# Two transformer blocks on one core: the second block's weight halves are made during the first block's feed-forward stage and kept in DRAM

## The chip, the cores and the metric

The kernel runs on one core of a Trainium2 chip. A core has five engines with an instruction queue each: TensorE (PE, matrix products; its weight loads are listed as PEld), VectorE (DVE), ScalarE (ACT), GpSimd (POOL) and SyncE (SP, which here only issues DMAs), and 16 DMA engines that all queues share. The metric is the device time of one execution in microseconds (us), the median of the runs.

## The reference

One sequence of 512 tokens of width 1024, all in float32, goes through two different transformer blocks:

```
def reference(x, ...):
    x = first_block(x, ...)       # window attention + sparse attention, merge, w_out;
                                  # then the feed-forward stage with w_ffn_in, conv, gate, w_ffn_out
    return second_block(x, ...)

# second_block
h = rms_norm(x, norm_g)
proj = h @ w_in                                        # [512, 2464]
cq, ckv, kr, dq, dk, dv, mq, z = split(proj, IN_OFFSETS_2)
y_mla  = mla_branch(cq, ckv, kr, ..., w_uq, w_ukv)     # 8 heads, latent attention (MLA)
y_diff = diff_branch(dq, dk, dv, ...)                  # 4 heads, two softmax maps each
y_mem  = mem_branch(mq, mem, ...)                      # 4 heads over 256 memory tokens
y = concat([y_mla, y_diff, y_mem]) * silu(z)
return x + y @ w_out                                   # w_out: [1024, 1024]
```

In the kernel the second block's weights are `w_in_2` (1024 x 2464), `w_uq_2` (256 x 768), `w_ukv_2` (128 x 1024) and `w_out_2` (1024 x 1024), 15.6 MB as float32.

## The kernel before, in words

TensorE multiplies in a 32-bit format that is narrower than float32 (float32r). So each float32 operand is split into two float32r halves, H (the rounded value) and L (the rest), and each product is three: H*H, H*L and L*H. `mm3` issues them (L193, L197, L198).

Weights take this way: `wload` has SP load a raw float32 tile into one of two `raw` buffers (L122); `wsplit` copies it to `wH` on ACT (L129) and subtracts to get `wL` on DVE or POOL, whichever `self.leng` names (L130). wH and wL have three buffers each of 128 x 1024. `dense_steps` computes transposed outputs, a tile of 128 features x 512 tokens at a time (24 products of 512 columns where the depth is 1024); `nat_steps` computes token-major outputs. Such tiles are collected in PSUM in two banks (tag `mm`, bufs=2), so a tile's result must be read out before the next but one begins.

The first block ends with its output product (`wo`) and the feed-forward stage `ffn`, in two halves: 11 pairs of u and g tiles of `w_ffn_in` each (22 tiles; DVE multiplies the PSUM bank by the token's factor at L959 (`cv`), a three-tap convolution follows on ACT and DVE (`cc`, L960 to L962), a gate and a split (`ct`, `aL`)), then eight tiles of `w_ffn_out` (`fo`).

The second block makes its latents (`lat`), stores the residual in token-major form, makes the queries and keys (`nat`, `uq`, `ukv`), norms and rotates them on DVE and POOL (`head_stat` L1060, `rsqrt` L267 to L274, `head_scale` L1069, `rope` L1090 on POOL, L1094 and L1096 on DVE), and runs three attentions, one behind the other in `pipeline`, with the gates `z` (eight tiles of 128 columns of `w_in_2`, L1464 to L1470) and the first half of the output product as fillers between their steps. The last half of the output product comes at the end. With `POOLL = 14`, `self.leng` is POOL from L1452 on and in the fillers of the attention, elsewhere DVE.

The program is written as generators that `weave` runs side by side; a scheduler then sets each engine's order from a list of priorities. On each engine, and on SP's queue, instructions run strictly in that order.

## Time and profile before

| | |
|---|---|
| runs | 1107.42, 1115.65, 1118.71 us; median 1115.65 |
| span of the profiled execution | 1107.7 us |
| mean clock granted to TensorE | 0.987 of full speed |
| busy in the span | PE 1049.2, DVE 759.3, ACT 579.9, POOL 267.8 us |
| HBM | 100.49 MB read, 10.77 MB written |

The median of the runs lies 8 us above the span of the profiled execution. By time, the first block's attention ends at about 396 us, its output product at 443, the feed-forward stage's first half at about 607, its second half at 803; the second block's latents and residual follow until 836, its queries and keys until 890, then the attentions until about 1071 and the end of the output product. Busy times are sums over an engine's instructions where they don't overlap; the share of busy time in the whole span hides that each stage has another limit, so the table by stretches is read stage by stage. "[5.34 <-POOL wL L130]" behind a row means that the engine was idle for 5.34 us before it, and what released it.

### The profile page before, as it was taken

Reading aid. Unit: us, or ns where it says so; the run is one execution under the profiler, and the core shown is the slowest. Engines: PE = TensorE matmul, PEld = TensorE weight load, DVE = VectorE, ACT = ScalarE, POOL = GpSimd, SP = SyncE. Lnnn points to the kernel's source line nnn. Section 1 sums busy time; section 2 is a strip of 40 time slices with the busy share of each in tenths; the row PEclk is TensorE's granted clock in tenths of the full one; section 3 lists DMA queues with packets and bytes.
Section 4 is the critical chain, followed back from the end, with each engine's and each line's share of the span. In section 5 each row is a group of like instructions: output and inputs, shape, how many; then the busy total and the mean of one; then the engine's idle time right before and its main releaser. Section 6 shows DMA issues by size and latency. Waiting matters only on the chain.

```text
span 1107.7 us, 15081 instructions
## 1 busy us (share of the span) xinstructions
PE 1049.2 (95%) x5425; PEld 872.8 (79%) x5425; DVE 759.3 (69%) x1553; ACT 579.9 (52%) x1098; POOL 267.8 (24%) x380
## 2 busy tenths in 40 slices
PE   5999989999999999999999999999999959999898
PEld 4797777877878878888888888888889947776688
DVE  6669884577872655777753477874454898988983
ACT  6557664577772444444432344445546527876640
POOL 4423134222220064000000200002410558331400
PEclk9999999999999999999999999999999979999999
DMA  7844345222114252232222423222333321264222
GB/s 184 273 115 156 100 102 136 43 48 43 49 44 113 77 181 88 76 114 84 83 81 78 151 90 101 76 81 79 110 97 109 96 57 39 89 179 143 68 66 77
DMA packets 105194, 110.14 MB, mean 99 GB/s; under 512 B 5508, under 2 KB 96106, under 8 KB 105120
## 3 DMA queue, kind: packets, MB, share of 16 engines
q1 hardware_dynamic: 101184, 98.81, 30.6%
q0 software_dynamic: 3936, 10.37, 3.1%
q8 instruction: 43, 0.70, 0.3%
q14 instruction: 31, 0.25, 0.1%
HBM read 100.49 MB, written 10.77 MB: 100 GB/s over the span
## 4 chain that ended last, share of the span: by engine, by line
PE 70%; DVE 15%; DMA 6%; ACT 4%; issue 3%; SPq 0%; POOL 0%; ACTq 0%; DVEq 0%; POOLq 0%
PE ps_mm L193 18%; PE ps_mm L197 18%; PE ps_mm L198 18%; DMA raw<-in_w_in 5%; PE ps_S L1241 3%; PE ps_T L383 3%; DVE wL L130 2%; PE ps_O L1272 1%; DMA xt<-in_x 1%; PE ps_O L1270 1%; DVE PTL L102 1%; ACT wH L129 1%; DVE e L372 1%; DVE rt L1094 1%; DVE e L1615 1%
## 5 line engine op out<-in xcount | busy, mean ns | idle before, releaser
L129 ACT ACTIVATE wH<-raw 128x1024 fp32r<-128x1024 f32 (+5 forms) x178 | 169.4, 953 | 260.9 <-PE ps_mm L197 207.8
L130 DVE TENSOR_TENSOR wL<-raw,wH 128x1024 fp32r<-128x1024 f32 (+5 forms) x150 | 166.6, 1112 | 116.5 <-ACT wH L129 116.1
L198 PE MATMUL ps_mm<-nH,wL 128*128 128x512 f32 x440 | 173.4, 394 | 5.3 <-POOL wL L130 5.3
L193 PE MATMUL ps_mm<-nH,wH 128*128 128x512 f32 x440 | 174.0, 395 | 0.0
L197 PE MATMUL ps_mm<-nL,wH 128*128 128x512 f32 x440 | 173.5, 394 | 0.0
L374 ACT ACTIVATE e<-e,mn 128x256 f32<-128x256 f32 (+5 forms) x160 | 86.4, 541 | 33.5 <-DVE mn L372 32.4
L198 PEld LDWEIGHTS ps_mm<-nH,wL 128*128 128x128 f32 x440 | 83.4, 189 | 22.6 <-POOL wL L130 5.8
L197 PEld LDWEIGHTS ps_mm<-nL,wH 128*128 128x128 f32 x440 | 83.5, 190 | 16.5
L193 PEld LDWEIGHTS ps_mm<-nH,wH 128*128 128x128 f32 x440 | 83.6, 190 | 16.2
L193 PE MATMUL ps_mm<-hH,wH 128*128 128x512 f32 x232 | 93.9, 405 | 0.0
L198 PE MATMUL ps_mm<-hH,wL 128*128 128x512 f32 x232 | 92.1, 397 | 0.0
L197 PE MATMUL ps_mm<-hL,wH 128*128 128x512 f32 x232 | 91.6, 395 | 0.0
L130 POOL TENSOR_TENSOR wL<-raw,wH 128x1024 fp32r<-128x1024 f32 (+1 forms) x28 | 60.8, 2170 | 76.5 <-ACT wH L129 63.3
L383 PE MATMUL ps_T<-ident,e 128*128 128x128 f32 x368 | 64.3, 282 | 11.4 <-DVE PTL L102 7.2
L101 ACT ACTIVATE PTH<-ps_T 128x512 fp32r<-128x512 f32 (+1 forms) x108 | 55.6, 528 | 32.6 <-PE ps_T L383 32.1
L102 DVE TENSOR_TENSOR PTL<-ps_T,PTH 128x512 fp32r<-128x512 f32 (+1 forms) x108 | 63.9, 606 | 12.3 <-ACT PTH L101 11.6
L193 PE MATMUL ps_mm<-aH,wH 128*128 128x512 f32 x176 | 69.5, 395 | 0.0
L198 PE MATMUL ps_mm<-aH,wL 128*128 128x512 f32 x176 | 69.5, 395 | 0.0
L197 PE MATMUL ps_mm<-aL,wH 128*128 128x512 f32 x176 | 69.5, 395 | 0.0
L383 PEld LDWEIGHTS ps_T<-ident,e 128*128 128x128 f32 x368 | 45.4, 143 | 28.7 <-DVE PTL L102 8.8
L958 POOL MEMSET cv<- 128x2 f32 x44 | 4.2, 99 | 237.1 <-DVE cc L962 230.5
L959 DVE TENSOR_TENSOR cv<-ps_mm,rB 128x512 f32<-128x512 f32 x44 | 30.3, 688 | 32.5 <-PE ps_mm L198 31.3
(550 smaller groups left out, 2544.0 us busy)
## 6 DMA issues: line engine op xcount, KB each, us to landing
raw<-in_w_ffn_in SPq DMA_DIRECT2D x20, 1024.0 KB, 5.2
raw<-in_w_in SPq DMA_DIRECT2D x16, 1024.0 KB, 6.9
raw<-in_w_in SPq DMA_DIRECT2D x16, 512.0 KB, 4.0
raw<-in_w_ffn_out SPq DMA_DIRECT2D x8, 768.0 KB, 4.7
raw<-in_w_ffn_out SPq DMA_DIRECT2D x8, 640.0 KB, 4.2
xt<-in_x SPq DMA_DIRECT2D x8, 512.0 KB, 4.9
raw<-in_w_out SPq DMA_DIRECT2D x4, 1024.0 KB, 5.2
raw<-in_w_out SPq DMA_DIRECT2D x8, 512.0 KB, 3.5
```

The lines of the kernel that those rows point to most:

```text
L101: nc.scalar.activation(H, src, AF.Copy)
L102: nc.vector.tensor_sub(L, src, f32(H))
L129: self.nc.scalar.activation(H, raw, AF.Copy)
L130: self.leng.tensor_sub(L, raw, f32(H))
L193: ins = mm(ps, wH, xH, start=first, stop=False)
L197: mm(ps, wH, xL, start=False, stop=False)
L198: mm(ps, wL, xH, start=False, stop=last)
L372: nc.vector.tensor_tensor_reduce(e, ps, bias, op0=ALU.add, op1=ALU.min, scale=1.0, scalar=3e38, accum_out=mn)
L374: nc.scalar.activation(e, e, AF.Exp, scale=-1.0, bias=mn, accum_out=sm)
L383: nc.tensor.transpose(ps[:, 128 * i:128 * i + 128], blk, self.ident)
L959: nc.vector.tensor_tensor(v[:, 2:], ps, rB, op=ALU.mult)
L1241: nc.tensor.matmul(ps[:, :n], q[:, 128 * b:128 * b + 128], k[:, :n], start=i == 0, stop=i == len(prods) - 1)
```

## The change

A list `later()` names 32 pieces of the second block's weights, mostly of 128 x 1024. A generator `presplit()` loads each into an SBUF tile `pre` (tag "e", two buffers, shared with the attention's strips), splits it in chunks of 512 columns into `preH` (ACT) and `preL` (DVE) with four buffers each, and stores both to DRAM, a piece later, 256 KB a store. `ffn` steps it behind gate and output tiles and drains it at the end. The second block then has no `wload` and `wsplit`: `fetch()` loads the ready halves from DRAM, for three of five pieces into wH and wL with a DMA each, for two of five into the two `raw` buffers with one DMA. `stream()` asks for a piece one ahead of its use (two ahead for the gates and the last half of the output product). The lines that set `self.leng` to POOL ahead of the attention are gone.

```
+    def presplit(self):
+        ...
+        def load(i):
+            key, n, w, pieces = specs[i]
+            t = self.work.tile([128, 1280], F32, tag="e", name="pre", bufs=2)[:, :n * w]
+            tv = t.rearrange("p (k c) -> p k c", k=n)
+            for o, pw, src in pieces:
+                nc.sync.dma_start(tv[:, :, o:o + pw], src)
+            return t
+        nxt = load(0)
+        yield
+        for i, (key, n, w, _) in enumerate(specs):
+            t = nxt
+            nxt = load(i + 1) if i + 1 < len(specs) else None
+            for d, st in ready:
+                nc.sync.dma_start(f32(d), f32(st))
+            ready = []
+            dst = self.dram.tile([128, 2, n * w], F32R, name="pre_" + "_".join(map(str, key)))
+            for o in range(0, n * w, 512):
+                m = min(512, n * w - o)
+                H = self.work.tile([128, 512], F32R, tag="PTH", name="preH", bufs=4)
+                L = self.work.tile([128, 512], F32R, tag="PTL", name="preL", bufs=4)
+                self.split(t[:, o:o + m], H[:, :m], L[:, :m])
+                ready += [(dst[:, 0, o:o + m], H[:, :m]), (dst[:, 1, o:o + m], L[:, :m])]
+            self.held[key] = (dst, n, w)
+            yield
+    def fetch(self, key):
+        dst, n, w = self.held.pop(key)
+        self.turn = getattr(self, "turn", -1) + 1
+        if self.turn % 5 < 3:
+            T = [self.wp.tile([128, n * w], F32R, tag=t, name=t, bufs=3) for t in ("wH", "wL")]
+            for i in range(2):
+                self.nc.sync.dma_start(f32(T[i]), f32(dst[:, i]))
+        else:
+            t = self.wp.tile([128, 2, n * w], F32R, tag="raw", name="wHL", bufs=2)
+            self.nc.sync.dma_start(f32(t), f32(dst))
+            T = [t[:, i] for i in range(2)]
+        return [t.rearrange("p (k c) -> p k c", k=n) for t in T]
...
     def ffn(self, last):
+            pre = self.presplit()
...
                     self.dense(Wi, [(0, 8)], 128 * (FT + i0 + i), 128 * n, self.nH, self.nL, gate)
+                    if hf or i > 2:
+                        next(pre)
+                        if i % 4:
+                            next(pre)
...
                     if hf:
                         last(m, x1)
+                    next(pre, None)
+                    if not hf:
+                        next(pre, None)
...
+            self.drain(pre)
...
-        if POOLL & 8:
-            self.leng = nc.gpsimd
...
-            yield from self.dense_steps(lambda k0, k1, c, w: W(k0, k1, 1440 + 128 * ZO[c // 128], w), [(0, 8)], 0, D,
-                                        self.nH, self.nL, ev, chunk=128)
+            yield from self.dense_steps(None, [(0, 8)], 0, D, self.nH, self.nL, ev, chunk=128,
+                                        pre=self.stream((("z", i) for i in range(8)), 2))
```

What this does to the order of instructions is seen at three places. On DVE in the feed-forward stage's first half, two u tiles stand like this before (`cv` reads the product out of PSUM, `cc` is the convolution, `wL` a half of the weights of the tile after):

```order
L959 TENSOR_TENSOR cv<-ps_mm,rB 128x512
L130 TENSOR_TENSOR wL<-raw,wH 128x1024
L961 SCALAR_TENSOR_TENSOR cc<-cv,vec_norm_ffn,cc 128x512
L962 SCALAR_TENSOR_TENSOR cc<-cv,vec_norm_ffn,cc 128x512
L959 TENSOR_TENSOR cv<-ps_mm,rB 128x512
```

and of the change, at the same place:

```order
L1057 TENSOR_TENSOR cv<-ps_mm,rB 128x512
L137 TENSOR_TENSOR wL<-raw,wH 128x1024
L1059 SCALAR_TENSOR_TENSOR cc<-cv,vec_norm_ffn,cc 128x512
L109 TENSOR_TENSOR preL<-pre,preH 128x512
L1060 SCALAR_TENSOR_TENSOR cc<-cv,vec_norm_ffn,cc 128x512
L109 TENSOR_TENSOR preL<-pre,preH 128x512
L1057 TENSOR_TENSOR cv<-ps_mm,rB 128x512
```

Two subtractions of a piece stand between a tile's `cv` and the next one's; in the 22 tiles there are 41.

On SP's queue in the same stage the loads of `w_ffn_in` follow each other in the kernel before, nine of 1 MB in a row:

```order
L122 DMA raw<-in_w_ffn_in 128x8x256
L908 DMA xt_3963<-in_x 128x4x256
L122 DMA raw<-in_w_ffn_in 128x8x256 x9
L122 DMA raw<-in_w_ffn_in 128x8x128 x2
L122 DMA raw<-in_w_ffn_out 128x6x256
```

and of the change, from one of these loads to behind the next:

```order
L129 DMA raw<-in_w_ffn_in 128x8x256
L191 DMA pre_nat_0_5587<-preL 128x512
L191 DMA pre_nat_0_5587<-preH 128x512
L191 DMA pre_nat_0_5587<-preL 128x512
L183 DMA pre<-in_w_in 128x4x256
L191 DMA pre_nat_4_5645<-preH 128x512
L191 DMA pre_nat_4_5645<-preL 128x512
L191 DMA pre_nat_4_5645<-preH 128x512
L191 DMA pre_nat_4_5645<-preL 128x512
L129 DMA raw<-in_w_ffn_in 128x8x256
L183 DMA pre<-in_w_in 128x4x256
```

A load and seven stores of pieces stand between two loads of the stage's own weights. The 124 stores in all are issued ahead of the first load of the feed-forward stage's second half.

On POOL where the queries `qn` and keys `kn` of the second block are rotated, the kernel before has weight halves between the rotation products:

```order
L130 TENSOR_TENSOR wL<-raw,wH 128x1024
L1090 TENSOR_TENSOR rt_7727<-qn,cc_mla_qn_g_5669 128x256
L1090 TENSOR_TENSOR rt_7746<-qn,cc_mla_qn_g_5669 128x256
L130 TENSOR_TENSOR wL<-raw,wH 128x1024
L1090 TENSOR_TENSOR rt_7769<-qn,cc_mla_qn_g_5669 128x256
L130 TENSOR_TENSOR wL<-raw,wH 128x1024 x2
L1090 TENSOR_TENSOR rt_7880<-kn,cc_mla_kn_g_5678 128x256
```

and of the change:

```order
L1197 TENSOR_TENSOR rt_8170<-qn,cc_mla_qn_g_5973 128x256
L1197 TENSOR_TENSOR rt_8189<-qn,cc_mla_qn_g_5973 128x256
L1197 TENSOR_TENSOR rt_8212<-qn,cc_mla_qn_g_5973 128x256
L1197 TENSOR_TENSOR rt_8317<-kn,cc_mla_kn_g_5982 128x256
L1197 TENSOR_TENSOR rt_8336<-kn,cc_mla_kn_g_5982 128x256
```

The halves are gone from POOL, here and in the attention behind it, 13 in all.

## Rows read from the trace of the kernel before

**Rows 1.** The page, busy us, share of the span and instructions by engine.
```profile
PE 1049.2 (95%) x5425; PEld 872.8 (79%) x5425; DVE 759.3 (69%) x1553; ACT 579.9 (52%) x1098; POOL 267.8 (24%) x380
```

**Rows 2.** Table by stretches: from:to, length, busy (instructions) by engine, clock, DMA share, GB/s.
```profile
443.00:550.00 107.00, 106.91 (x475) 88.26 (x476) 82.82 (x122) 46.15 (x58) 1.89 (x19) 1.00 0.29 93
870.00:890.00 20.00, 20.00 (x169) 20.00 (x168) 19.85 (x42) 7.61 (x14) 10.06 (x6) 1.00 0.21 53
890.00:900.00 10.00, 4.66 (x22) 3.75 (x22) 9.75 (x21) 1.34 (x3) 3.92 (x3) 0.73 0.14 31
900.00:910.00 10.00, 5.07 (x21) 3.80 (x20) 8.68 (x24) 4.07 (x7) 5.45 (x5) 0.84 0.28 75
910.00:920.00 10.00, 8.75 (x32) 7.35 (x33) 6.52 (x14) 4.56 (x12) 9.76 (x14) 0.57 0.00 1
920.00:960.00 40.00, 38.70 (x238) 32.03 (x237) 37.41 (x98) 33.65 (x82) 20.17 (x27) 1.00 0.19 54
960.00:1050.00 90.00, 79.70 (x419) 62.87 (x417) 80.77 (x185) 61.78 (x159) 33.42 (x28) 0.96 0.44 132
```

**Rows 3.** Timeline of PE: start us, us, instruction, idle before and its releaser.
```profile
897.46 0.79 PE L198 MATMUL ps_mm<-nH,wL 128*128 128x512 f32 x1 [5.34 <-POOL wL L130]
...
901.46 0.40 PE L198 MATMUL ps_mm<-nH,wL 128*128 128x512 f32 x1
...
910.47 1.09 PE L1511 MATMUL ps_mm<-ident,kn 128*96 128x128 f32 x4 [5.40 <-DVE z L1464]
```

**Rows 4.** Timeline of DVE, 869 to 905 us.
```profile
869.12 0.96 DVE L1096 TENSOR_TENSOR qn<-rt,rt 128x256 f32<-128x256 f32 x1 [2.97 <-POOL rt L1090]
870.00 2.48 DVE L1094 TENSOR_TENSOR rt<-qn,sn_mla_qn_g 128x128 f32<-128x128 f32 x1
...
873.61 3.25 DVE L1094 TENSOR_TENSOR rt<-qn,sn_mla_qn_g 128x128 f32<-128x128 f32 x2
...
883.34 2.42 DVE L273 TENSOR_TENSOR rsq<-rsq 128x32 f32<-128x32 f32 x1
...
890.83 0.28 DVE L1094 TENSOR_TENSOR rt<-kn,sn_mla_kn_g 128x128 f32<-128x128 f32 x1
...
894.39 3.17 DVE L1094 TENSOR_TENSOR rt<-kn,sn_mla_kn_g 128x128 f32<-128x128 f32 x2
...
900.55 3.63 DVE L1069 TENSOR_TENSOR mq<-mq,hf 128x256 f32<-128x256 f32 x4
```

**Rows 5.** Groups by line, 850 to 1108 us: count, busy us, mean ns, idle before.
```profile
L130 POOL TENSOR_TENSOR wL<-raw,wH 128x1024 fp32r<-128x1024 f32 x13 | 33.5, 2579 | 32.1 <-ACT wH L129 28.7 <-PE ps_T L383 3.3
```

**Rows 6.** Timeline of POOL, two of these halves.
```profile
883.27 2.44 POOL L130 TENSOR_TENSOR wL<-raw,wH 128x1024 fp32r<-128x1024 f32 x1 [6.57 <-ACT wH L129]
...
895.01 2.40 POOL L130 TENSOR_TENSOR wL<-raw,wH 128x1024 fp32r<-128x1024 f32 x1
```

**Rows 7.** Waits of PE, 780 to 1108 us: us in total, times, longest.
```profile
PE ps_T L383 <- DVE PTL L102: 6.5, 3, 3.6
```

**Rows 8.** Groups of DVE by line, shapes apart, 445 to 540 us.
```profile
L130 DVE TENSOR_TENSOR wL<-raw,wH 128x1024 fp32r<-128x1024 f32 x18 | 22.0, 1223 | 2.1 <-ACT wH L129 2.1
...
L102 DVE TENSOR_TENSOR aL<-ct,aH 128x512 fp32r<-128x512 f32 x8 | 5.5, 685 | 0.0
```

**Rows 9.** Table by stretches, the one with the highest DMA share.
```profile
1010.00:1020.00 10.00, 9.21 (x46) 6.51 (x44) 9.09 (x27) 6.14 (x21) 1.31 (x1) 1.00 0.94 307
```

**Rows 10.** The page, DMA issues: count, KB each, median us to landing.
```profile
raw<-in_w_ffn_in SPq DMA_DIRECT2D x20, 1024.0 KB, 5.2
...
raw<-in_w_in SPq DMA_DIRECT2D x16, 512.0 KB, 4.0
...
raw<-in_w_up_a SPq DMA_DIRECT2D x4, 512.0 KB, 6.2
...
xf_d<-z SPq DMA_DIRECT2D x8, 256.0 KB, 4.4
...
raw<-in_w_in SPq DMA_DIRECT2D x2, 304.0 KB, 9.9
```

More of the change, by code (lines that the diff above doesn't have):

```diff
@@ L131, in wsplit, with later, columns @@
         return H, L
+    def later(self):
+        a = self.a
+        W, Q, U, O = (self.rows(a[n][0] if len(a[n].shape) == 3 else a[n]) for n in ("w_in_2", "w_uq_2", "w_ukv_2", "w_out_2"))
+        out = [(("lat", m), 8, 128, [(0, 128, W(0, 8, 128 * m, 128))]) for m in range(3)]
+        def columns(name, src, k0, k1, cols):
+            for i, pieces in enumerate(cols):
+                w = sum(p[1] for p in pieces)
+                n = 1024 // w
+                for k in range(k0, k1, n):
+                    kk = min(k + n, k1)
+                    o, ps = 0, []
+                    for c0, pw in pieces:
+                        ps.append((o, pw, src(k, kk, c0, pw)))
+                        o += pw
+                    out.append(((name, i, k), kk - k, w, ps))
+        columns("nat", W, 0, 8, NAT[:1])
+        columns("uq", Q, 0, 2, UQ)
+        columns("ukv", U, 0, 1, UKV)
+        for i in range(1, len(NAT)):
+            for k in (0, 4):
+                out.append((("nat", i, k), 4, 256, [(0, 256, W(k, k + 4, NAT[i][0][0], 256))]))
+        out += [(("z", i), 8, 128, [(0, 128, W(0, 8, 1440 + 128 * m, 128))]) for i, m in enumerate(ZO)]
+        for k in (0, KO):
+            for i in range(4):
+                out.append((("out", i, k), 4, 256, [(0, 256, O(k, k + 4, 256 * i, 256))]))
+        return out
@@ L134, in weave, with stream @@
+    def stream(self, keys, ahead=1):
+        keys = list(keys)
+        q = []
+        for i in range(len(keys)):
+            while keys and len(q) <= ahead:
+                q.append(self.fetch(keys.pop(0)))
+            yield q.pop(0)
     @staticmethod
@@ L209, in weights @@
         def weights(i, gi):
+            if pre is not None:
+                return next(pre)
             c, o = tiles[i]
@@ L1026, in nat_steps @@
                 k1 = min(k1, k0 - kb + kr)
-                H, L = self.wsplit(raw[:, kb:kb + k1 - k0])
+                H, L = next(pre) if pre is not None else self.wsplit(raw[:, kb:kb + k1 - k0])
                 if own:
@@ L1719, in block2 @@
         yH, yL = [None] * 8, [None] * 8
-        Wout = self.rows(a["w_out_2"][0])
         def ysplit(ms):
@@ L1730, in late_fill @@
             nonlocal xo
-            def weights(i):
-                return self.wsplit(self.wload(Wout(0, KO, 256 * i, 256), KO, 256))
+            pre = self.stream(("out", i, 0) for i in range(4))
             n = 0
@@ L1779, in block2 @@
         self.leng = v
-        self.nat(Wout, 8, [(256 * i, 256) for i in range(4)], yH, yL, fin, tail=True, kf=KO)
+        self.nat(None, 8, [(256 * i, 256) for i in range(4)], yH, yL, fin, tail=True, kf=KO,
+                 pre=self.stream((("out", i, KO) for i in range(4)), 2))
         late.close()
```

39 lines of the change are left out of this document (25 added, 14 removed).

## The prediction

> **What bounds the kernel now.** I read the page first: TensorE is busy for 1049.2 of the 1107.7 us [rows 1], so at most some 58 us, plus what the clock loses, can be won without taking products away. The table by stretches then says where these 58 us lie. In the first block's feed-forward stage (FFN) there are none: TensorE is busy for 106.91 of 107 us [rows 2]. Apart from the first block's beginning, the holes are in the second block, from 890 us on: 4.66 of 10 us busy in 890 to 900, 5.07 in 900 to 910, 38.70 of 40 in 920 to 960 and 79.70 of 90 in 960 to 1050 [rows 2]. The clock falls in the same places, to 0.73, 0.84 and 0.57 of full speed in three stretches of 10 us [rows 2].
>
> TensorE's timeline has two holes in 890 to 911. The first ends at 897.46, after 5.34 us of waiting for a weight half made by POOL (wL, L130), and the product behind it takes 0.79 us, at half the clock, against 0.40 from 901.46 on. The second ends at 910.47, after 5.40 us on DVE (z, L1464), where the keys of the latent attention (MLA) are turned [rows 3]. The wait on z is one by name only: z stands on DVE behind everything that it does for the queries and keys, and DVE is busy for 19.85 of 20 us in 870 to 890, 9.75 of 10 after that and 8.68 of 10 in 900 to 910 [rows 2]. So DVE sets the date at which attention begins.
>
> Why DVE is so late is in its own timeline. The rotation product `rt` of L1094 takes 0.28 us at 890.83, but 2.48 at 870.00; two of them take 3.25 at 873.61 and 3.17 at 894.39; a Newton step of L273 on 32 columns takes 2.42 at 883.34; four L1069 take 3.63 at 900.55; and 2.97 us pass idle before 869.12, on a POOL product [rows 4]. POOL makes 13 weight halves in the second block, 33.5 us in all, 2579 ns each [rows 5]; those at 883.27 and 895.01, for two, take 2.44 and 2.40 us [rows 6], as long as the DVE rows that they overlap are too long. I read this as DVE held by POOL: an instruction that should take 0.2 to 0.6 us takes 2.2 more.
>
> **What the change removes.** All 13 POOL halves, those of DVE and the copies on ACT leave the second block.
> - Before the attention, POOL has six halves. Five hold DVE for some 2.2 us each (2.48 - 0.28 at 870.00, 2.42 - 0.2 at 883.34, 3.17 - 0.56 at 894.39, and likewise at 873.61 and 900.55), 11 us, and in the idle 2.97 POOL is stuck in one [rows 4]. That is 14 us of DVE's chain, which would end near 896 instead of 910. TensorE gets the first gate's weights without the wait of 5.34 [rows 3] and is through with that tile at about 897, so that both engines arrive together: the keys are turned near 898, 12 us earlier. The clock of 0.57 in 910 to 920 [rows 2] costs up to 4 us of its 8.75 busy ones; with no hole ahead I take 2 of them back. Together 14 us.
> - In the attention POOL has seven halves, at 2.2 us up to 15 us of DVE time, and DVE's own halves there, a good 1 us each, go too. DVE is busy for 37.41 of 40 and 80.77 of 90 us there [rows 2], but TensorE idles for only 1.3 and 10.3. TensorE's three waits on PTL (6.5 us, [rows 7]) are of this kind. Nothing won is the lower end, 11.6 the upper; I take 7.
> - From 803 to 860 nothing goes that TensorE waits for long; I count 1 us. Gain: 14 + 7 + 1 = 22 us.
>
> **What it adds.** 32 pieces of weights are loaded, split in chunks of 512 columns (one ACT copy `preH`, one DVE subtraction `preL`) and stored, 256 KB a store. The order of the changed kernel shows all of it between the first block's output product and the end of the FFN's first half; the second half has none.
> - *DVE.* In the 22 u and g tiles there stand 41 `preL`, 1.9 a tile. A tile is 24 products; 475 take 106.91 us, so 5.40 us a tile, of which DVE has 82.82/107, or 4.18 us [rows 2]. A subtraction of this shape from SBUF (aL, L102) takes 0.685 us [rows 8], about 0.60 where rows overlap as those of DVE do. 1.9 of them are 1.1 to 1.3, so DVE stands at 5.3 to 5.5 us a tile: 98 to 101%. It was 77%. The tiles' halves wL (1.22 us, [rows 8]) and the evacuation of PSUM stand behind `preL` on the same engine, and the products have two PSUM banks, so TensorE stops once DVE is a tile late.
> - *ACT* has 46.15 of 107 us there [rows 2], 2.33 a tile; even at DVE's 0.685 us a copy it comes to 3.6 of 5.4: not the bound.
> - *DMA.* In the middle of the stage, five 1 MB weight loads on SP's queue have 8 pieces and 32 stores between them: 5.24 + 4.19 + 8.39 = 17.8 MB in ten tiles, 54 us, or 330 GB/s. The most that the trace shows is 307 GB/s at a share of 0.94 [rows 9], which would be 326 at full share. So DMA also stands at 100%. Over the whole stage it is 41.0 MB from the first FFN load (about 410) to 552, at 326 GB/s 126 of 142 us: what is late in the middle is made good at the ends, through two raw buffers and three of wH and wL.
> - *The loads of the pieces.* Each is asked for one piece ahead, some 5.9 us (22 tiles for 20 pieces). 512 KB takes 4.0 us in the lighter stages, 6.2 in that of w_up_a, and w_in's first pieces took 9.9 in the rush at the start; the FFN's own 1 MB takes 5.2, a 256 KB store of block two 4.4 [rows 10]. Past 5.9 us each piece holds ACT and DVE by the excess, and all that is queued behind.
>
> The bounds of this cost are zero (98% fits) and 20 x (9.9 - 5.9) = 80 us less one tile of cover. I choose 6.5 us for the landing, near the 6.2 of the busiest stage with such loads: 20 x 0.6 = 12, less one tile of 5.4, is 7, and 1 for DVE over its limit: 8 us. The fetches of block two double its reads: 1 MB for each tile of 5.4 us against 5.2 us to land, one tile ahead (two for the gates): hidden, 0 us; without that cover 5.2 us at each of three tiles of latents.
>
> The Trainium skill speaks against this change: "DMA: Bandwidth & Descriptors" (Measured) asks for transfers of 1 MiB or more, and "SBUF — State Buffer" (The DMA setup-cost knee) has 224 GB/s at 256 KiB and 341 at 1 MiB. By these, 18.6 MB of stores and 22.4 MB of loads are an estimated 83 + 66 = 149 us, over the 142 that there are. The trace's 307 GB/s is of several transfers in flight, which no lone transfer shows; the sum above goes by it.
>
> **Sum.** 1107.7 - 22 + 8 = 1093.7 in the profiled execution's terms. The median of the runs, 1115.65, lies 8 us above that execution's span, so 1101.7 us.
>
> **Rivals.**
> - *A, the sum:* 1094 to 1106; 0.40.
> - *B, the FFN hides everything* (landings under 5.9 us, `preL` filling DVE's idle fifth): no loss, the gain 22 to 28: 1088 to 1094, say 1092. For it: TensorE at 100% has never had to wait there, DVE's idle time is there to be used. Against it: 98 to 101%. 0.20.
> - *C, the first half of the FFN becomes bound by DVE or DMA* by a sixth of its 119 us: 20 us, 1115.65 - 22 + 20 = 1114. For it: both at 100% in the middle, small stores. 0.17.
> - *D, only the hole ahead of the attention is won*, since attention is a chain through TensorE, ACT and DVE where a faster DVE waits elsewhere: 15 - 8 = 7, 1109. For it: TensorE's named waits in 910 to 1108 are short. Against it: DVE at 90 to 94%. 0.10.
> - *E, slower:* pieces land in 8.5 us as in the rush at the start. 20 x 2.6 - 5.4 = 47 us against 22: 1140. It decides from 7.8 us on, where the loss passes gain and 11 us. For it: a queue in order, in which a piece waits behind seven stores. Against it: no landing in the FFN is over 5.2 us at its share of 0.29 [rows 2, 10]. 0.13.
>
> **The numbers.** This kernel's runs differ by 1% (1107.42 to 1118.71), about what a measurement can tell from no change: faster is under 1104.5, slower over 1126.8. A (but for 0.04 of it) and B are faster, 0.56; C, D and that rest are the same, 0.31; E is slower, 0.13. The range 1086 to 1125 leaves out E and the best of B; A alone is 1094 to 1106.
>
> **What would show it.** After the change: no POOL weight halves beyond 800 us, `rt` of L1094's kind under 0.6 us throughout, no half-clock products after the first gate, keys turned some 12 us earlier after the second block's start. In the FFN's first half TensorE falls under 100%, about 8 us in all, waiting on DVE (wL or cv) that waits on ACT that waits for `pre`; DMA share near 0.9 there against 0.29, DVE over 95%. Wrong would be: TensorE at 100% there (B), holes of 15 us or more (C, E), or DVE rows of 2 us and more in 860 to 910 with POOL empty of halves, which would mean that POOL's halves weren't what held DVE.

## The result, and the profile after

The changed kernel takes 1121.21 us (median of 20 runs, 1112.67 to 1129.89), the kernel before 1113.53 us in the 20 runs beside it (1107.42 to 1119.82). The ratio is 1.0053, 95% interval 1.0035 to 1.0070: the change makes the kernel some 4 to 8 us slower, where 14 us faster was forecast. It lies in the range (1086 to 1125), outside that of case A (1094 to 1106), between rivals C (1114) and E (1140).

One correction first. In every execution whose time and span are both on record the time is some 1.7 us above the span. So the profiled execution of before, with its span of 1107.7 us, stands for a time of about 1109.4 us, 4 below the median of the 20. There are no 8 us around a span, and its span set against a later one flatters before by some microseconds. They show at once: tile 2 (counted from 0) of the first block's output product, which stands ahead of all that the change touches, already starts 1.5 to 8.9 us later in every later trace than in that of before.

The page of the changed kernel, busy time by engine (answers [rows 1]):

```profile
PE 1054.6 (94%) x5425; PEld 878.6 (78%) x5425; DVE 748.5 (67%) x1595; ACT 583.4 (52%) x1127; POOL 232.6 (21%) x367
```

Its table by stretches for the first block's output product (from 396 us) and feed-forward stage (FFN), and then for the second block from the end of the FFN to the turning of the keys and from there to the end (columns as in [rows 2], which this answers):

```profile
396.00:443.00 47.00, 30.95 (x136) 24.35 (x136) 17.11 (x25) 13.97 (x21) 27.79 (x43) 0.85 0.50 150
443.00:550.00 107.00, 103.05 (x443) 83.68 (x443) 83.78 (x133) 58.02 (x87) 1.36 (x15) 0.95 0.88 285
550.00:650.00 100.00, 92.55 (x384) 73.49 (x383) 69.24 (x99) 48.22 (x70) 12.23 (x30) 0.97 0.93 301
650.00:800.00 150.00, 150.00 (x659) 123.46 (x658) 103.85 (x134) 61.18 (x78) 1.89 (x19) 1.00 0.31 99
...
846.00:938.90 92.90, 92.57 (x636) 87.08 (x634) 54.60 (x177) 39.84 (x81) 18.86 (x24) 1.00 0.59 197
...
938.90:1122.30 183.40, 172.25 (x1084) 147.55 (x1084) 141.21 (x375) 102.44 (x268) 46.42 (x61) 0.99 0.40 128
```

The stretch of the output product and the same two stretches of the second block in the kernel before:

```profile
396.00:443.00 47.00, 47.00 (x221) 37.96 (x220) 25.29 (x33) 21.38 (x31) 30.39 (x43) 1.00 0.35 113
...
803.00:910.40 107.40, 95.16 (x636) 88.28 (x634) 75.14 (x189) 53.76 (x100) 32.79 (x29) 0.96 0.32 92
...
910.40:1107.70 197.30, 179.37 (x1084) 151.26 (x1084) 161.27 (x383) 114.37 (x280) 65.55 (x69) 0.96 0.30 93
```

The reader sees a trade. The second block does the same 636 and 1084 products in 92.9 + 183.4 us instead of 107.4 + 197.3: 28.4 us won, more than the 22 forecast. The output product and the FFN's first half, where TensorE missed nothing before (47.00 of 47 us, and 106.91 of 107 in [rows 2]), lose more than that: 30.95 of 47 us busy from 396 on, then 103.05 of 107 and 92.55 of 100, at a clock of 0.85, 0.95 and 0.97.

**Where the time is lost.** The table follows the same instructions through the traces: how much later each starts than in the trace of before, for the changed kernel and for the experiments on it below. Each column is read from one execution.

| us later than before at | before | after | e1 | e2 | e3 | e4 | e5 | e6 | e7 | e9 | e10 |
|---|---|---|---|---|---|---|---|---|---|---|---|
| output product, x of tile 2 | 409.04 | 5.7 | 3.4 | 8.1 | 1.9 | 6.4 | 6.4 | 6.3 | 1.5 | 8.9 | 2.6 |
| output product, x of tile 7 | 439.22 | 23.6 | 3.4 | 8.1 | 1.9 | 6.4 | 6.4 | 6.3 | 1.4 | 8.9 | 2.6 |
| FFN, first cv | 449.52 | 30.5 | 9.1 | 8.1 | 1.8 | 6.4 | 6.4 | 6.3 | 1.4 | 8.9 | 2.6 |
| FFN, cv of tile 21 | 560.00 | 41.0 | 20.6 | 15.8 | 6.1 | 15.3 | 11.1 | 37.2 | 1.4 | 8.9 | 12.8 |
| FFN, last x | 802.92 | 43.1 | 23.5 | 19.1 | 29.9 | 20.8 | 13.0 | 60.8 | 1.4 | 11.7 | 14.3 |
| keys turned | 910.47 | 28.4 | 8.9 | 4.4 | 15.2 | 6.1 | -1.7 | 46.2 | -13.3 | -3.0 | -0.3 |
| end of the span | 1107.7 | 14.6 | -5.0 | -8.9 | 1.3 | -5.5 | -15.1 | 31.4 | -26.9 | -17.1 | -7.5 |
| **lost by the end of the FFN** (row 5 - row 1) | | 37.4 | 20.1 | 11.0 | 28.0 | 14.4 | 6.6 | 54.5 | 0 | 2.8 | 11.7 |
| **won after it** (row 5 - row 7) | | 28.5 | 28.5 | 28.0 | 28.6 | 26.3 | 28.1 | 29.4 | 28.3 | 28.8 | 21.8 |

The changed kernel loses 37.4 us in two places, and only the second had a term in the sum: 18 us between tiles 2 and 7 of the output product, then 19.5 us in the FFN (6.9 up to the first cv, 10.5 in the 22 tiles, 2.1 behind them; `cv` is DVE's, and with two banks TensorE can be up to a tile ahead of it, so this split of the 19.5 is rough).

The first place is one wait. Timeline of SP's queue around it (start us, us, instruction), of the changed kernel:

```profile
401.87 0.37 SPq L129 DMA_DIRECT2D raw<-in_w_out  x1
406.99 0.37 SPq L1006 DMA_DIRECT2D xt<-in_x  x1
429.48 2.58 SPq L183 DMA_DIRECT2D pre<-in_w_in  x2
432.16 0.53 SPq L129 DMA_DIRECT2D raw<-in_w_ffn_in  x1
```

and its waits on SP's queue from 390 to 660 us (engine, line, what it waited for, us in total, times, longest):

```profile
SPq L183 <- DVE preL L109: 34.6, 15, 5.2
SPq L183 <- POOL turns L1241: 22.1, 1, 22.1
```

The first load of a piece, L183, writes a `pre` tile, which takes a buffer of tag "e". Both of that tag's buffers were still held by POOL, which makes the second block's rotation tables with scratch tiles of that tag. POOL's timeline:

```profile
425.58 3.88 POOL L1241 TENSOR_TENSOR turns<-turns,e 128x64 f32<-128x64 f32 x10
```

These ten end at 429.46, the last of them the last reader of one buffer, and the load goes out at 429.48. Behind it in the queue stands a weight load of the FFN, issued at 432.16. And ACT and DVE have the first piece's split in their orders at the same place; their timelines, with PE's:

```profile
433.57 1.15 ACT L108 ACTIVATE preH<-pre 128x512 fp32r<-128x512 f32 x2 [19.57 <-DMA pre<-in_w_in]
```

```profile
434.23 1.29 DVE L109 TENSOR_TENSOR preL<-pre,preH 128x512 fp32r<-128x512 f32 x2 [18.85 <-ACT preH L108]
...
439.66 0.68 DVE L1016 SCALAR_TENSOR_TENSOR x<-ps_mm,x 128x512 f32<-128x512 f32 x1
```

```profile
440.39 0.80 PE L289 MATMUL ps_mm<-mH,wH 128*128 128x512 f32 x1 [15.29 <-DVE x L1016]
```

`x` (L1016) reads the output product out of PSUM. TensorE had nothing more to do from 440.39 - 15.29 = 425.10 on, until this bank was read; but `x` stands on DVE behind `preL`, which waits for `preH`, which waits for the load, which waits for POOL. TensorE's next product then takes 0.80 us, against 0.39 before the wait: it runs at half the clock.

The second place is the one that was foreseen, but larger. Waits of ACT from 390 to 660 us in the changed kernel, those of `preH`:

```profile
ACT preH L108 <- DMA pre<-in_w_in: 22.2, 3, 19.6
ACT preH L108 <- DMA pre_nat<-preH: 18.7, 8, 4.2
ACT preH L108 <- DMA pre_z<-preH: 12.8, 8, 4.5
ACT preH L108 <- DMA pre_out<-preH: 7.7, 4, 3.5
ACT preH L108 <- DMA pre_lat<-preH: 4.8, 4, 1.8
```

and DMA issues from 440 to 650 us (count, KB each, median us to landing; answers [rows 10]):

```profile
pre<-in_w_in SPq DMA_DIRECT2D x14, 512.0 KB, 7.1
pre_z<-preH SPq DMA_DIRECT2D x16, 256.0 KB, 6.3
...
pre_nat<-preH SPq DMA_DIRECT2D x15, 256.0 KB, 7.8
```

Leaving out the one wait of 19.6 us, `preH` waits 2.6 us for loads of `w_in` (and 2.4 for those of `w_out`) but 44.0 us (18.7 + 12.8 + 7.7 + 4.8) for stores: the four `preH` buffers come free only when a store has landed, 6 to 8 us after it was issued. What reaches TensorE stands in its own waits from 443 to 660 us:

```profile
PE ps_mm L289 <- ACT aH L108: 4.8, 3, 2.6
PE ps_T L346 <- DVE preL L109: 3.3, 1, 3.3
PE ps_mm L289 <- ACT wH L136: 1.5, 1, 1.5
PE ps_mm L289 <- DVE cv L1057: 1.5, 2, 1.2
```

ACT takes its instructions in order, so a `preH` that waits holds `aH` and `wH` behind it. The loss is not idle time alone: TensorE idles for 11.4 us of the 207 from 443 to 650 (3.95 + 7.45), and the clock of 0.95 and 0.97 is worth about 8 more (0.05 x 107 + 0.03 x 100, an estimate from the rounded means). Together that is the 19.5.

DVE's 83.78 of 107 us are 78% of that stretch, but its first 37 us are still the output product. From the first `cv` to the 22nd, 480.1 to 601.0 us, DVE is busy for 103.89 of 120.90 us, 86%, or 4.95 us a tile, where the prediction had 5.3 to 5.5 and 98 to 101%.

### The profile page after: what moved, and what is told of

It reads as the page before. It is cut to its first block, busy times and chain, and to the rows that moved or that the text cites. A ratio compares the mean times of both kernels' runs of the same rounds, so it can differ in the third digit from the quotient of the medians.

```text
span 1122.3 us, 15417 instructions
## 1 busy us (share of the span) xinstructions
PE 1054.6 (94%) x5425; PEld 878.6 (78%) x5425; DVE 748.5 (67%) x1595; ACT 583.4 (52%) x1127; POOL 232.6 (21%) x367
## 4 chain that ended last, share of the span: by engine, by line
PE 63%; DVE 13%; DMA 13%; ACT 4%; issue 3%; POOL 3%; SPq 1%; POOLq 0%; ACTq 0%; DVEq 0%
PE ps_mm L289 15%; PE ps_mm L294 15%; PE ps_mm L293 15%; DMA raw<-in_w_in 4%; DVE wL L137 3%; PE ps_S L1348 3%; PE ps_T L481 2%; DMA pre_nat<-preH 2%; DMA pre_z<-preH 2%; PE ps_O L1377 1%; DMA xt<-in_x 1%; PE ps_O L1379 1%; DVE PTL L109 1%; PE ps_S L294 1%; PE ps_S L289 1%
## 5 line engine op out<-in xcount | busy, mean ns | idle before, releaser
L136 ACT ACTIVATE wH<-raw 128x1024 fp32r<-128x1024 f32 (+4 forms) x145 | 136.9, 945 | 183.9 <-PE ps_mm L293 145.1
L137 DVE TENSOR_TENSOR wL<-raw,wH 128x1024 fp32r<-128x1024 f32 (+4 forms) x130 | 144.4, 1112 | 85.6 <-ACT wH L136 85.1
L289 PE MATMUL ps_mm<-nH,wH 128*128 128x512 f32 x416 | 165.3, 397 | 6.1 <-ACT aH L108 2.3
L294 PE MATMUL ps_mm<-nH,wL 128*128 128x512 f32 x416 | 164.7, 396 | 0.0
L293 PE MATMUL ps_mm<-nL,wH 128*128 128x512 f32 x416 | 164.1, 394 | 0.0
L472 ACT ACTIVATE e<-e,mn 128x256 f32<-128x256 f32 (+5 forms) x160 | 86.3, 541 | 26.9 <-DVE mn L470 25.9
L289 PEld LDWEIGHTS ps_mm<-nH,wH 128*128 128x128 f32 x416 | 79.3, 191 | 24.8 <-ACT aH L108 3.0
L294 PEld LDWEIGHTS ps_mm<-nH,wL 128*128 128x128 f32 x416 | 79.2, 190 | 16.5
L293 PEld LDWEIGHTS ps_mm<-nL,wH 128*128 128x128 f32 x416 | 79.3, 191 | 16.0
L109 DVE TENSOR_TENSOR PTL<-ps_T,PTH 128x512 fp32r<-128x512 f32 (+1 forms) x108 | 63.8, 606 | 14.0 <-ACT PTH L108 12.2
L108 ACT ACTIVATE preH<-pre 128x512 fp32r<-128x512 f32 (+3 forms) x62 | 37.0, 608 | 69.2 <-DMA pre<-in_w_in 22.2
L109 DVE TENSOR_TENSOR preL<-pre,preH 128x512 fp32r<-128x512 f32 (+3 forms) x62 | 40.9, 667 | 46.7 <-ACT preH L108 29.6
```

Of the source, the lines that this page charges most:

```text
L108: nc.scalar.activation(H, src, AF.Copy)
L109: nc.vector.tensor_sub(L, src, f32(H))
L136: self.nc.scalar.activation(H, raw, AF.Copy)
L137: self.leng.tensor_sub(L, raw, f32(H))
L289: ins = mm(ps, wH, xH, start=first, stop=False)
L293: mm(ps, wH, xL, start=False, stop=False)
```

## Experiments

Two theories of the loss stood against each other: that a shared buffer holds the queue once and the crowding of DMA costs the rest, or that the FFN is bound throughout by an engine (DVE, as in the prediction's rival C) or by the stores' bytes. For the gain: POOL holds DVE, or DVE was merely relieved of its own halves.

**e1, the rotation tables with buffers of their own.** The rest of the edit keeps the first loads at their place on SP's queue, behind the same load of `xt`; further back single rows of the queue change places, so the order is nearly that of the changed kernel and not row for row the same.

```diff
-            q, n = (self.work.tile([128, 1280], F32, tag="e", name="e", bufs=2)[:, :64 * n_]
+            q, n = (p.tile([128, 64 * n_], F32, name=f"tab{_}")
...
+                ins = nc.sync.dma_start(tv[:, :, o:o + pw], src)
+                if i == 0:
+                    self.tc.keep_in_program_order(ins)
...
+            next(pre)
-                    if hf or i > 2:
+                    if hf or i > 4:
```

> The changed kernel with one difference: the two scratch tiles of the rotation tables (POOL) get buffers of their own, so that the first loads of pieces need not wait until POOL is done with the tables; the order of SP's queue stays row for row. Theory W (the load that waits for the tables' buffer holds SP, ACT and DVE, and so TensorE): the wait of 22 us on SP and the hole of 15.3 us in TensorE go, with the half-clock stretch behind it; 18 to 25 us less than the changed kernel, ratio to before 0.98 to 0.99, and the loss of 10 to 13 us in the u and g tiles stays. Theory C (DVE and DMA are overfull, the wait only shows it early): the pieces come earlier and crowd the output product instead; less than 8 us won, ratio 0.998 or more.

1105.00 us (9 runs), ratio 0.9903 (0.9873 to 0.9932). The wait for `x` is gone: the lag is 3.4 us both at tile 2 and at tile 7 of the output product, where the changed kernel's grows by 18 us; the first load goes out at 405.18 us, right behind `xt` at 404.76, and DVE still has four `preL` ahead of the next `x`. The 20 us of crowding stay (3.4 to 23.5). So the shared buffers cost the 18 us (e2 agrees), which alone turn the change from a gain of 1% into a loss.

**e2, the first load held back to its place in the program.** The scheduler had moved it forward on SP's queue, to where the tables still hold its buffers; `keep_in_program_order` forbids that for this one DMA. The pieces then begin in the FFN.

```diff
+                ins = nc.sync.dma_start(tv[:, :, o:o + pw], src)
+                if i == 0:
+                    self.tc.keep_in_program_order(ins)
```

> The changed kernel, but the first load of a piece keeps its place behind what the program has on SP's queue before it, so that no piece is loaded before the tenth u or g tile; nothing is taken away. Theory W: no wait for the tables, TensorE full in the output product; the crowding comes later and reaches into the second half of the stage; loss 5 to 12 us in all against 37 now, ratio to before 0.975 to 0.985. Theory C: the same pieces in a shorter place cost TensorE as much as before, 12 us and more from the tenth tile on, ratio 0.99 to 1.0.

1099.24 us (4 runs), ratio 0.9858 (0.9788 to 0.9929). No loss before the FFN, 11.0 us in it, 28.0 won behind it. It is the base of the experiments that follow.

**e3, every load held to its place.**

```diff
-                nc.sync.dma_start(tv[:, :, o:o + pw], src)
+                self.tc.keep_in_program_order(nc.sync.dma_start(tv[:, :, o:o + pw], src))
```

> The changed kernel, but each load of a piece keeps its place on SP's queue as the program has it, so the 32 pieces spread over both halves of the feed-forward stage. Theory W and the crowding term of my sum together: DVE at 77% plus 9% and DMA at 0.29 plus 0.3 leave TensorE nearly full; loss 0 to 4 us, gain of 28 us in the second block kept: ratio to before 0.975 to 0.98 (25 us). If each wait of a piece on its load costs TensorE wherever it stands (loads late), the loss stays at 10 us or more: ratio 0.985 to 0.99.

1114.83 us (10 runs), ratio 0.9989 (0.9964 to 1.0013): a miss, since the loss grew to 28.0 us. Up to the first half's 22nd tile it is only 4.2 (1.9 to 6.1); 24 us are lost in and just behind the eight output tiles, where the program takes 16 of its steps through the 32 pieces. Its stretch there, and the waits, on PE from 396 to 800 us and on SP from 440 to 720:

```profile
550.00:650.00 100.00, 84.27 (x337) 66.00 (x336) 56.25 (x79) 42.10 (x63) 7.09 (x24) 0.91 0.94 307
```

```profile
PE ps_mm L289 <- ACT wH L136: 10.8, 2, 7.0
PE ps_mm L289 <- ACT aH L108: 6.3, 2, 4.3
```

```profile
SPq L191 <- ACT preH L108: 46.0, 11, 6.5
```

A store (L191) that stands at the head of SP's queue waits for ACT to make its half, and the FFN's own weight load behind it waits too; 46 us of such waits, and TensorE's longest waits are for wH. That the queue in order hurts here, without any buffer of the tables, is how I read it; DMA is also at a share of 0.94, and e3 does not separate the two.

**e4, DVE's share of the split cut to a sixteenth**, on top of e2.

```diff
-                self.split(t[:, o:o + m], H[:, :m], L[:, :m])
-                ready += [(dst[:, 0, o:o + m], H[:, :m]), (dst[:, 1, o:o + m], L[:, :m])]
+                nc.scalar.activation(H[:, :m], t[:, o:o + m], AF.Copy)
+                nc.vector.tensor_sub(L[:, :32], t[:, o:o + 32], f32(H[:, :32]))
+                ready += [(dst[:, 0, o:o + m], H[:, :m]), (dst[:, 1, o:o + m], H[:, :m])]
```

> As the kernel with the first load held, but DVE subtracts only 32 of each 512 columns of a piece, and the store of the L half takes the H half instead (the second block's weights are then not the right ones); DMA and ACT do the same as there. If the loss in the crowded u and g tiles is DVE's (98 to 101% busy), it falls from tile ten on to under a third of that of the kernel with the first load held; if it is DMA's (0.9 busy, loads and buffers late), it stays.

1103.86 us in a single run, without an interval. The loss is 14.4 us, not less than e2's 11.0. The edit did more than it was meant to: both stores of a chunk now read `preH`, so each of its buffers is held by two stores, and ACT's waits for stores from 390 to 720 us are 63.5 us against e2's 44.0. So e4 alone doesn't clear DVE; e5 below does.

**e5, a sixteenth of the stores' bytes**, on top of e2: as many stores, loads and splits.

```diff
+            if i == 0:
+                one = self.dram.tile([128, 2, n * w], F32R, name="pre_one")
+            c = 512 if i == 0 else 32
...
+                z = o if i == 0 else o // 16
+                ready += [(dst[:, 0, z:z + c], H[:, :c]), (dst[:, 1, z:z + c], L[:, :c])]
+            self.held[key] = (one[:, :, :n * w], n, w)
```

> As the kernel with the first load held, but from the second piece on only 32 columns of each half of a chunk are stored (a sixteenth of the bytes, the same number of stores), and the second block reads one stored piece for all its weights (which are then not the right ones). Loads, splits and SP's order stay. If the loss of 11 us after the tenth tile is that of DMA (31 MB of stores, landing in 6 to 8 us, that hold the four buffers of preH), ACT's waits on stores (44 us) fall below 10 and the loss to 0 to 4 us. If it is SP's queue or the splits on ACT and DVE, it stays at 8 and more.

1094.32 us in a single run. The loss falls from 11.0 to 6.6 us, between the two outcomes that were expected (0 to 4, or 8 and more). ACT's waits from 390 to 660 us:

```profile
ACT preH L108 <- DMA pre<-in_w_in: 14.6, 10, 2.6
...
ACT preH L108 <- DMA pre_out<-preH: 7.3, 4, 3.8
...
ACT preH L108 <- DMA pre_nat<-preH: 4.1, 3, 1.6
```

ACT's waits for stores fall from 44 us to some 16, not below 10. By these two traces the stores' bytes are some 40% of the loss; their effect through the buffers of `preH` and through the load on DMA isn't separated. TensorE is busy for 106.95 of 107 us from 443 to 550 with DVE at 91.73 us, 86%: DVE carries the splits and the stage's own work and is not full.

**e6, the stores on POOL's queue**, on top of e2, so that no load stands behind a store.

```diff
-                nc.sync.dma_start(f32(d), f32(st))
+                nc.gpsimd.dma_start(f32(d), f32(st))
```

> As the kernel with the first load held, but POOL issues the stores instead of SP; nothing else differs, bytes and splits least of all. If the queue costs the time (stores that wait on SP for their half, with weight loads behind them), the loss of 11 us falls to 0 to 4 and the ratio to before is 0.975 to 0.98. If the bytes cost it, the loss stays at 8 to 14 us, ratio 0.983 to 0.99.

1141.76 us (4 runs), ratio 1.0222 (1.0178 to 1.0265): a miss, and the slowest kernel of all, with 54.5 us lost in the FFN. Its table by stretches, and a wait of ACT from 390 to 720 us:

```profile
550.00:600.00 50.00, 39.17 (x146) 31.17 (x147) 37.17 (x56) 25.76 (x41) 18.92 (x42) 0.86 0.97 297
600.00:650.00 50.00, 38.55 (x142) 28.06 (x140) 25.76 (x37) 19.51 (x31) 29.61 (x57) 0.89 0.96 330
```

```profile
ACT preH L108 <- DMA pre<-in_w_in: 42.2, 14, 7.7
ACT preH L108 <- DMA pre<-in_w_out: 23.3, 8, 4.7
```

DMA is at a share of 0.97 and 0.96, and TensorE at 39 of 50 us. More than the queue differs: the pieces stand closer together (62 splits between 483 and 659 us, where e2 has them between 485 and 693), and ACT waits for their loads instead of for stores. The stores themselves land no later than in e2 (5.3 to 6.7 us against 6.2 to 7.5, medians of the 256 KB stores of `lat`, `nat`, `z` and `out`), but the stage's own `w_ffn_out` does, in 8.1 and 10.9 us from 440 to 700 against 6.5 and 5.8. I read this as the pieces crowding out the stage's own loads, once no load stands behind a store; no run moves the stores to POOL at e2's density, so that stays argued. The second queue adds little throughput: 297 and 330 GB/s, where e2 has 303 from 550 to 650. The Trainium skill, "Trainium Kernel Development and Optimization" (Key Constraints), says that DMAs from the SP, ACT and POOL queues share the same 16 engines, and that several issuers save issue time only; the run's throughput agrees. It goes further than the page: here the kernel with the second queue is 3.7% slower than e2, by their ratios to the kernel before.

**e7, the second block's gain alone.** On top of e2, one piece is made and stored, and every fetch reads from it; the FFN has no pieces otherwise.

```diff
-        specs = self.later()
+        specs = self.later()[:1]
...
-            self.held[key] = (dst, n, w)
+            for key, n, w, _ in self.later():
+                self.held[key] = (dst[:, :, :n * w], n, w)
```

> The second block of the changed kernel without the cost: one piece alone is split and stored, and each load of ready halves reads that one (the weights are then not the right ones); what is read, when and how much stays. My gain of 22 us in the second block would give a ratio to before of 0.98; the 28 us that the traces show between the first block's end and the end, 0.975. If the gain in the trace were the run's own good luck, 0.985 or more.

1085.48 us (4 runs), ratio 0.9726 (0.9686 to 0.9765), and nothing lost in the FFN (lag 1.5 at its start, 1.4 at its end). The gain is 28.3 us by the table, 26 to 35 by the ratio's interval. The doubled reads of the second block cost nothing that shows: no wait of TensorE for a DMA stands in the changed kernel's trace behind 846 us. With e7 as the kernel without a loss, the ratios give the losses a second time, from all the runs: some 36 us for the changed kernel (0.0327 x 1114), 20 for e1, 15 for e2, 29 for e3 and 55 for e6, near the table's 37.4, 20.1, 11.0, 28.0 and 54.5. The intervals are 3 to 8 us wide either way, so the differences among e2, e4, e5 and e10 (6.6 to 14.4 us, one trace each) are not clear of those between executions of one kernel.

**e8 and e11, the kernel before with POOL's halves on DVE.** This is no part of the change: it tests alone whether POOL's halves held DVE. e8 moves the six halves ahead of the attention, e11 all 13; DVE then has more work, not less.

```diff
-POOLL = 14
+POOLL = 6
```

> The kernel before, with one number changed, so that the weight halves between the queries' rotation and the attention are made by DVE instead of POOL; those in the attention stay on POOL. DVE then has six halves of 1.2 us more, 7.3 us. If POOL's halves held DVE (2.2 us each and 3 of idle, 14 in all), DVE's chain ends 6 to 7 us earlier, no rotation product takes over 0.6 us, and the time is 5 to 8 us less, ratio 0.993 to 0.995. If they did not, it ends 7 us later, ratio 1.005 or more.

```diff
-POOLL = 14
+POOLL = 2
```

> The kernel before with no weight half of the second block on POOL: DVE makes those of the attention too, 7 more at 1.2 us. If POOL's halves hold DVE by 2.2 us each in the attention as ahead of it, DVE is 7 us better off and the time falls by 2 to 6 us against the kernel with only the earlier ones moved (ratio 0.991 to 0.995). If DVE's own load is what limits the attention, the 8 us more that it does itself make it no better: ratio 0.997 to 1.0, and the changed kernel's gain there is that of the work taken away.

e8: 1110.28 us (10 runs), ratio 0.9965 (0.9937 to 0.9994), 1 to 7 us less than before where 5 to 8 were expected; the keys are turned at 910.90, 0.4 us later than before after a start 5.0 us later, so 4.6 us are won up to there, with six more halves on DVE (7.3 us by the expectation). DVE's timeline of e8 where [rows 4] had 2.48, 3.25 and 2.42:

```profile
872.28 0.28 DVE L1094 TENSOR_TENSOR rt<-qn,sn_mla_qn_g 128x128 f32<-128x128 f32 x1
...
873.69 1.02 DVE L1094 TENSOR_TENSOR rt<-qn,sn_mla_qn_g 128x128 f32<-128x128 f32 x2
...
883.35 0.19 DVE L273 TENSOR_TENSOR rsq<-rsq 128x32 f32<-128x32 f32 x1
...
906.66 2.29 DVE L273 TENSOR_TENSOR rsq<-rsq 128x64 f32<-128x64 f32 x1
```

The long rows are gone, but for one at 906.66, beside one of the seven halves that POOL still makes.

e11: 1099.37 us (4 runs), ratio 0.9842 (0.9797 to 0.9886), more than expected: with one number changed and nothing precomputed, the kernel is 1.6% faster than before and 2% faster than the changed one. In the attention, two of DVE's groups by line before (912 to 1041 us; count, busy us, mean ns):

```profile
L1470 DVE SCALAR_TENSOR_TENSOR z<-zt,z 128x512 f32<-128x512 f32 x7 | 9.5, 1361 | 0.9 <-ACT zt L1465 0.7
...
L1691 DVE TENSOR_SCALAR e<-e,sm 128x256 f32<-128x256 f32 x8 | 8.5, 1102 | 0.0
```

In e11 (913 to 1042 us) these means are 706 ns and 344 ns. So POOL's halves did hold DVE, and moving them to DVE wins 15.6 us (the lag falls from 6.4 to -9.2) of the 28 that the change wins in the second block: 4.8 up to the turning of the keys, of the change's 14.7, and 10.8 behind it, of 13.8. The other 13 go with the work that the change takes away and e11 does not, all the halves on DVE and the copies on ACT; no run divides them further. The Trainium skill, "SBUF — State Buffer" (Who interferes with whom), says that a VectorE instruction with two inputs in SBUF contends with a GpSimd instruction that reads SBUF. The rows of `rt` and `rsq` agree, 2.48 and 2.42 us with POOL in a half, 0.28 and 0.19 without.

**e9, the pieces spread over the whole FFN.** Loads, splits and stores all stay where the program has them, and the program steps them on five of nine u and g tiles of both halves, after the third tile, and once per output tile.

```diff
-                nc.sync.dma_start(tv[:, :, o:o + pw], src)
+                keep(nc.sync.dma_start(tv[:, :, o:o + pw], src))
...
-                self.split(t[:, o:o + m], H[:, :m], L[:, :m])
+                keep(nc.scalar.activation(H[:, :m], t[:, o:o + m], AF.Copy))
+                keep(nc.vector.tensor_sub(L[:, :m], t[:, o:o + m], f32(H[:, :m])))
...
+                if tiles[0] > 2 and tiles[0] % 9 % 2 == 0:
+                    next(pre, None)
+                tiles[0] += 1
-                    if hf or i > 2:
-                        next(pre)
-                        if i % 4:
-                            next(pre)
-                    if not hf:
-                        next(pre, None)
```

> The changed kernel with its pieces spread by hand: one step about every second u or g tile from the fourth on, and one for each output tile, over both halves of the feed-forward stage; loads, splits and stores keep the program's place on their queues, so a store is issued a step (some 11 us) after its split. Theory: pieces cost TensorE where DMA is at its limit or a queue waits for a late half; at 1.5 MB a step in 11 us (0.29 + 0.42 = 0.7 of DMA) neither happens: loss 0 to 5 us, gain 28 to 30 kept, ratio to before 0.972 to 0.98. If waits of ACT on its piece cost TensorE at any density, the loss stays at 10 us or more, ratio 0.983 or more.

1090.80 us (4 runs), ratio 0.9752 (0.9695 to 0.9809): the fastest kernel that does all the work, by the ratios 3% below the changed one. Its table by stretches:

```profile
443.00:550.00 107.00, 106.91 (x480) 87.99 (x479) 87.09 (x131) 52.95 (x73) 1.85 (x20) 1.00 0.56 174
550.00:650.00 100.00, 98.31 (x423) 78.56 (x422) 57.30 (x80) 39.91 (x57) 9.46 (x27) 1.00 0.83 253
650.00:800.00 150.00, 150.00 (x658) 123.03 (x657) 121.63 (x165) 86.29 (x124) 12.49 (x25) 1.00 0.76 238
```

The same bytes, the same splits and the same stores, at a DMA share of 0.56 to 0.83 instead of 0.88 to 0.93, cost 2.8 us (0.9752 against e7's 0.9726 says the same). e3, whose pieces also reach into the second half, but with 16 of 32 steps on eight tiles, has TensorE at 84.27 us and DMA at 0.94 in 550 to 650 and lost 28.0. That speaks for the spreading; e9 also holds splits and stores to their place, which e3 does not, and a dense kernel with all three held wasn't run, so the order's part isn't excluded.

**e10, 14 of the 32 pieces** (those of `nat` from the second on, and `z`), on top of e2; the others are split in the second block on ACT and DVE as before.

```diff
-        specs = self.later()
+        specs = [s for s in self.later() if s[0][0] == "z" or s[0][0] == "nat" and s[0][1]]
```

> As the kernel with the first load held, but only 14 of the 32 pieces (nat from the second group on, and the gates) are split early; the others are split in place by ACT and DVE when the second block asks for them, none by POOL. Bytes and splits in the feed-forward stage fall by half: loss 5 us instead of 11 if it goes with the bytes; the gain falls from 28 by about 1 us for each of the 4 output pieces split in the attention and 1 ahead of it: 23; ratio 0.984 with a 0.005 either way. If most of the gain were in the other pieces (DVE and ACT relieved in all of block two), ratio 0.99 or more.

1102.15 us (4 runs), ratio 0.9871 (0.9824 to 0.9918). It wins 21.8 us behind the FFN, but still loses 11.7 in it, as much as e2 with 32 pieces. By these traces the loss doesn't go with the number of bytes: the 14 pieces crowd the same tiles (a DMA share of 0.72 from 443 to 550 us, against e2's 0.69), and after that the lag stays. That agrees with e9: how densely pieces stand seems to decide, more than how many there are.

## Why the prediction was wrong

**The step that failed: the cost has no term for what the first load waits for.** "The order of the changed kernel shows all of it between the first block's output product and the end of the FFN's first half" is right, and "Each is asked for one piece ahead, some 5.9 us" was set against landings alone, as if a load could be issued when its turn comes. I read where the loads stand on SP's queue and how long they take, and not which buffer each writes and who still reads it. The section on the change says that `pre` shares tag "e"; that the rotation tables use that tag too, and that POOL is still making them until 430 us, stood in the code and in the trace of before. The wait of 22.1 us came from there, 18 us of it reached TensorE, and e1 took them away by giving the tables buffers of their own. The hole of 15.29 us is of the size that the prediction named as its sign of being wrong, but rivals C and E had it from other causes (engines full, slow landings); none had this one.

**The crowding of the FFN was mis-sized: 8 us foreseen, 19.5 measured** (11.0 where pieces begin later, e2). The term stood on the loads: 20 pieces x (6.5 - 5.9) us. The landing of 6.5 us was about right (6.7 us on the page, 7.1 in the stretch), but two terms were missing. The clock had none: of the 19.5 us about 11.4 are idle time and 8 products at the lower level behind the holes. And the stores had none: their landing holds the four buffers of `preH`, and ACT waited 44 us for them against 5 for loads. With a sixteenth of their bytes (e5) the loss was 4 us smaller. TensorE's named waits were more for ACT (`aH` and `wH`, 6.3 us) than for DVE (4.8), which was to be the one. The DMA share of 0.88 to 0.93 that was named as a sign came true.

**DVE as a limit was wrong, though its sum was not far off.** "DVE stands at 5.3 to 5.5 us a tile: 98 to 101%" came out at 4.95 us a tile, below the 5.40 that TensorE takes: between the first `cv` and the 22nd there were 34 `preL`, 1.6 a tile and not 1.9, since part of the 41 stand ahead of the first `cv`. DVE is 86% busy there, and in e5 it is 86% busy from 443 to 550 with TensorE at full work.

**The gain's mechanism was right, and its size before the attention too.** 15 us (14, and 1 for the start) were foreseen from the end of the first block's FFN to the turning of the keys; the lag falls by 14.7 us, and by 14.6 or 14.7 in each kernel of the table. TensorE's idle time there goes from 107.40 - 95.16 = 12.2 us to 0.3, and its busy time from 95.16 to 92.57 because the half-clock products are gone: the 12 us of the earlier keys and the 2 of the clock. DVE's timeline in the changed kernel has the short rows that were named as the sign ([rows 4] had 2.42, 3.17 and 3.63):

```profile
916.56 0.19 DVE L371 TENSOR_TENSOR rsq<-rsq 128x32 f32<-128x32 f32 x1
...
923.60 1.04 DVE L1201 TENSOR_TENSOR rt<-kn,sn_mla_kn_g 128x128 f32<-128x128 f32 x2
...
929.30 1.42 DVE L1176 TENSOR_TENSOR mq<-mq,hf 128x256 f32<-128x256 f32 x4
```

The sign held for the halves, not to the letter: one of the two `rt` at 923.60 still takes 0.8 us, over the 0.6 that was named, beside a rotation product of POOL.

**The term of the attention was mis-sized: 7 us foreseen, 13.9 measured** (197.30 to 183.40). The bound of 11.6 us was TensorE's idle time alone. Idle time did shrink as foreseen, from 17.93 to 11.15 us, by 6.8. The other 7.1 us are busy time, 179.37 against 172.25 for the same 1084 products at a clock of 0.96 and 0.99: products behind the small holes had run at half the clock, and the holes went. By these rounded means the clock is worth some 6 of the 7 (0.04 x 197.3 less 0.01 x 183.4, an estimate). I had a clock term for the stretch before the attention and none for the attention itself.

**The sum.** In spans: +5.7 at the start, which is no part of the change, +18 for the queue, +19.5 for the crowding, -28.5 in the second block, 14.7 in all by these rounded steps; the spans differ by 1122.3 - 1107.7 = 14.6. Without the start it is 9 us slower, and the medians say 7.7. With the forecast's 22 and 8 the sign was that of the gain; the missing 18 us turned it. And the 8 us that the prediction put around the span belong in no sum of this kernel.

**What stays open.** Of the crowding in e2, the stores' bytes are some 4 of 11 us (e5, a single run, and so not clear of noise); how the rest divides between the loads' landings and the stores' fixed time wasn't separated, nor density from order in e9. Nor was e9 tried with POOL's tables in buffers of their own, or with the stores in fewer, larger transfers.

## What to carry to other kernels

When work is moved forward in time, ask of its first DMA which buffer it writes and who still reads that buffer, because on a queue in order one load that waits holds every load behind it, and the split that waits for it holds every engine's order. When an idle resource is to be filled, spread the new work thinly and evenly over the whole stretch: the same 32 pieces cost 28 us with half of their steps on eight tiles, 11 us in dense sequence, and 2.8 us spread evenly over the stage. And where one engine's instruction is several times longer than its like, look at what POOL does in that moment before moving work between stages: changing one number won 1.6% here.

## What the runs showed of the hardware that I had not expected

- Most 256 KB stores from SBUF to DRAM land 5.8 to 7.8 us after their issue (medians by piece) at a DMA share of 0.9, and most 16 KB stores in e5 still take 3.0 to 4.5 us: a buffer that is freed by a store is held for longer than the split of a piece (1.15 us for two chunks on ACT) by far.
- DMA moved 285 to 301 GB/s at shares of 0.88 to 0.93 with loads of 512 KB and stores of 256 KB mixed, and 330 GB/s in one stretch of e6, where TensorE did least: throughput at the top is no sign that the loads which matter come in time.
- Small holes cost twice: of the 13.9 us won behind the turning of the keys, 7.1 were busy time, most of it products that had run at the lower of the two clock levels, though the mean granted clock rose by 0.03 only. In the changed kernel's FFN 11.4 us of idle time cost some 8 us of clock besides.
- POOL's subtraction of 128x1024 lengthens not only DVE's instructions with two tensors as inputs: the scaling of the strips (L1691, one tensor and a column) fell from a mean of 1102 to 344 ns when the halves left POOL; its two longest rows, 2.48 and 2.42 us, overlap halves of POOL.
